# Output projection of row blocks 0 to 3 placed among the last attention head's blocks 4 to 7

## The chip, the cores and the metric

The kernel runs on one core of one Trainium2 chip. Its time is the time of one execution in microseconds (us) on the device. Unchanged, it took 1444.61 us in the median of 3 runs, which lay between 1444.29 and 1447.48 us. One further execution was taken by the hardware profiler; all durations below are of that one.

## The reference, cut to what matters

The reference is one inference step of one hybrid decoder layer, in float32. A prompt of 1024 rows with 16 meta tokens in front goes through a norm and one input projection. Its columns feed two groups: differential attention (4 heads, each with two softmax maps whose difference weights V) and a gated causal convolution with a layer norm. Both are joined again by the output projection:

```
attn_out = diff_head_out(attn_o, lw, li)
conv_out = silu(layer_norm(conv_y, cln_w, cln_b))
mix = concatenate([attn_out, conv_out], -1) @ w_out
x = x_res + rms_norm(mix, ln_mix_post)
h = rms_norm(x, ln_ffn_pre)
f = (silu(h @ w_gate) * (h @ w_up)) @ w_down
return x + rms_norm(f, ln_ffn_post)
```

Beside it eight sample sequences take one decode step each over 4096 past positions, whose keys and values lie in 256 pages of 128 rows. The keys, values and the last convolution inputs are outputs too.

## The kernel before, in words

The prompt is worked in row blocks of 128 (eight of them). Every large matmul is computed from two halves of each operand, a rounded one (H) and the rest (L), by three matmuls of 512 columns (`mm3`, lines 148 to 151): H·H, H·L, L·H. So each weight must first be loaded (SyncE, the SP queue), cast to H on ScalarE (ACT) and have its L subtracted, for the output projection on GpSimd (POOL; lines 132, 138 and 140, tiles `wo0r`, `wo0H`, `wo0L` to `wo7`), for the FFN on VectorE (DVE; lines 947, 955, 957, tiles `wr`, `wH`, `wL`).

The stages follow each other on TensorE (PE): input projection with the convolution beside it; attention of 4 heads by 8 row blocks (`attn`); output projection of 8 row blocks (`c_block`); FFN over 22 slices of the hidden width, each with three weights (gate, up, down). The decode step's work is spread over all of this in small portions: page loads on SP (line 665), products with the keys on POOL (line 679), sums on DVE (line 689), matmuls with the values on PE (`pv`, line 731).

One attention block is this chain: scores `S` on PE (lines 507, 508), taken out of PSUM on DVE with the position bias and a running minimum (line 509), `exp` on ACT (line 515), the difference of the two maps on DVE (line 526), transposes `AT` on PE (line 534), copies `ats` on ACT (line 538), products with V into `o` on PE (line 548). After blocks 3 and 7 of a head, its four blocks are normed: ACT copies `oh` and sums squares (lines 557 to 562), POOL raises to the power -1/2 (`or`, line 564), ACT scales (line 566), and `head_out` transposes on PE (`oT`, line 571), scales on ACT (line 573) and, for heads 0 to 2, stores to `mixT`. Number `od` says at which block of the next four `head_out` of the last four is issued.

`c_block(b)` reads the mix of block b (`mx`, loaded from `mixT`; for the last head straight from the tile of line 573), casts and splits it (`mH` on ACT, `mL` on DVE, lines 899 and 900), does 48 matmuls `mo` in two halves of 24, and then a chain of small norm steps on DVE, ACT and POOL (lines 909 to 918).

In the program text a loop over n = 8·head + block issues `attn`, from n = `wo0` on two loads and splits of the output projection's weights per step, and from n = 24 + `c0` on one `c_block` per step; the remaining blocks follow behind the loop. A scheduler then orders each engine's queue by its own estimate of when things can run. `slabs` is the number of 128 x 1056 float32 buffers that weights, activations and most large tiles take turns in.

Of the kernel before, what the change touches and what calls it, by code (L numbers as in the profile page):

```python
# [46 lines left out]
def tile_layer(ctx: ExitStack, tc: tile.TileContext, I, O, cfg):  # L47
# [4 lines left out]
    cst = ctx.enter_context(tc.tile_pool(name="cst", bufs=1))  # L52
    dec = ctx.enter_context(tc.tile_pool(name="dec", bufs=2))
    sm = ctx.enter_context(tc.tile_pool(name="sm", bufs=4))
    at = ctx.enter_context(tc.tile_pool(name="at", bufs=cfg["at"]))
# [379 lines left out]
    def conv_norm(b):  # L435
        pt = pdec(f"yT{b}")
        for ct in range(4):
            T.transpose(out=pt[:, ct * P : (ct + 1) * P], in_=u[ct][:, 30 + b * P : 30 + (b + 1) * P], identity=ident)
        r, nb = ln_stats(pt[:, :], P, f"ln{b}")
        for ct in range(4):  # L440
            S.activation(
                u[ct][:, 30 + b * P : 30 + (b + 1) * P], pt[:, ct * P : (ct + 1) * P], AF.Identity, scale=r, bias=nb
            )

    def conv_act(ct, half):
        pt = pdec(f"zT{ct}{half}")
        a = 30 + 512 * half
        for b in range(4):
            T.transpose(out=pt[:, b * P : (b + 1) * P], in_=u[ct][:, a + b * P : a + (b + 1) * P], identity=ident)
        S.activation(u[ct][:, a : a + 512], pt, AF.Silu, scale=clnw[:, ct : ct + 1], bias=clnb[:, ct : ct + 1])  # L450
        if half == 1:
            S.dma_start(mixT[4 + ct], u[ct][:, 30 : 30 + SEQ])
# [335 lines left out]
    def dec_step(rate):  # L788
        owed[0] += rate
        n = int(owed[0])  # L790
        owed[0] -= n
        for _ in range(n):
            if dst["done"]:
                return
            with tc.high_priority(offset=-cfg["behind"]):
                try:
                    if next(dgen) == "wait":
                        return
                except StopIteration:
                    dst["done"] = True  # L800
# [41 lines left out]
    def w_out_load(k):  # L842
        wo.append(load_split(I["w_out"][0, k * P : (k + 1) * P, :], f"wo{k}", G, n3=False))
# [3 lines left out]
    def c_start():  # L847
        C["wpost"] = slab("wpost")
        bcast_row(C["wpost"][:, :DM], I["ln_mix_post"][0])
        C["wffn"] = slab("wffn")  # L850
        bcast_row(C["wffn"][:, :DM], I["ln_ffn_pre"][0])
        C["hT"] = {}
        C["h"] = {}
        C["in"] = {}
# [24 lines left out]
    def c_load(b):  # L879
        rs = slice(b * P, (b + 1) * P)  # L880
        mx = [att(f"mx{b}{i}") for i in range(2)]
        for i in range(2):
            n = 3 + i
            D.dma_start(kn(mx[i], n), mixT[4 * i : 4 * i + n, :, rs].rearrange("c p t -> p c t"))
        xr = slab(f"xr{b}")
        D.dma_start(xr[:, :DM], I["x_prompt"][0, rs, :])
        C["in"][b] = mx, xr
# [412 lines left out]
    def chunk_to(n):  # L1300
        while emitted[0] < min(n, total):
            next(fl)
            emitted[0] += 1
            if emitted[0] == total:
                for _ in fl:
                    pass
                v_out()
                sample_v()
                sample_k()

    def c_one(b):
        if b + 1 < NB:
            c_load(b + 1)
        c_block(b)
        if b == cfg["hb"]:
            hT_chunk(0)
            for x in range(min(b, 4)):
                h_transpose(x)
        elif cfg["hb"] < b < 5:
            h_transpose(b - 1)  # L1320
        if b == cfg["w0"]:
            w_raw(0)
            w_split(0)
        if b == cfg["w1"]:
            w_raw(1)
        dec_step(cfg["rate_c"])

    nwo, ncb = 0, 0
    for n in range(NH * NB):
        h, i = n // NB, n % NB  # L1330
        chunk_to(max(9 * h + (1 if i < 2 else 2 if i < 5 else 3), 1 + int(29 * n / cfg["fend"])))
        attn(h, i)
        if cfg["cn"] <= n < cfg["cn"] + NB:
            conv_norm(n - cfg["cn"])
        if n == cfg["cn"] + NB:
            for ct in range(4):
                for half in range(2):
                    conv_act(ct, half)
        if n == cfg["scn"]:
            sample_conv()  # L1340
        if n >= cfg["wo0"]:
            for _ in range(cfg["wor"]):
                if nwo < 8:
                    w_out_load(nwo)
                    nwo += 1
                    if nwo == 8:
                        c_start()
                        c_load(0)
        if n >= 24 + cfg["c0"] and ncb < 3:
            c_one(ncb)  # L1350
            ncb += 1
        if n >= cfg["db"]:
            dec_step(cfg["rate_b"][h])
# [28 lines left out]
CFG = dict(  # L1382
    nb=3, no=1, ns=6, nd=1, nc=2,
    sqv=1, ksp=0, asp=1, sps=1,
    od=1, kt=0, ho=0,
    wd='d',
    lag=7, rlag=1, elag=2,
    xn_g=(), wi_first=1, wi_e=(13, 17), sq=0,
    behind=-400, w0=7, w1=7, wi_n=1, anchor=1, wi_v=(8, 9, 10, 11, 12), taps=11, conv=400, r2_g=1, hb=5,
    vgrp=2, fing=5, ml_g=0, fend=22, cst=0, db=3, cn=6, scn=12, wo0=27, wor=2, c0=7,  # L1390
    at=8, slabs=35, kv=4, p=6, dve_mul=0, rate_b=(1, 1.25, 1, 0.75), rate_c=1, rate_d=2.45, rate_s=2.2,
    ffn_l=lambda nc: nc.vector,
)
_INS = [
# [16 lines left out]
def build_program(inputs):  # L1411
    import numpy as np
    import concourse.bacc as bacc

    nc = bacc.Bacc("TRN2", target_bir_lowering=False, num_devices=1, dynamic_dma_scratch_size=1024)
    arrays, I, O = {}, {}, {}
    for name in _INS:
        a = np.ascontiguousarray(inputs[name])
        arrays["in_" + name] = a
        I[name] = nc.dram_tensor("in_" + name, a.shape, mybir.dt.from_np(a.dtype), kind="ExternalInput").ap()  # L1420
    for name, shape in _OUTS:
        O[name] = nc.dram_tensor("out_" + name, shape, F32, kind="ExternalOutput").ap()
    with tile.TileContext(nc, schedule_with_timeline_sim=True, auto_bufs=True) as tc:
        tile_layer(tc, I, O, CFG)
    return nc, arrays
# [8 lines left out]
```

## Time and profile before

| | |
|---|---|
| median of 3 runs | 1444.61 us |
| profiled execution | 1442.33 us |
| its span, first to last instruction | 1440.6 us |
| mean granted TensorE clock (1 is full) | 0.976 |
| PE busy | 1353.5 us (94%), 6960 matmuls |
| DVE, ACT, POOL busy | 876.8, 552.2, 560.5 us |
| the chain that ended last: PE's share | 61% |

The profiled execution is 1.7 us longer than its span, and 2.28 us shorter than the median of the runs. The first output projection matmul starts at 451.51 us of the span, the FFN's first at 548.91 us. A matmul's row shows when it started and how long it ran; consecutive ones overlap, so that a stretch is read by starts.

### The profile page before, as it was taken

Reading aid. Unit: us, or ns where it says so; the run is one execution under the profiler, and the core shown is the slowest. Engines: PE = TensorE matmul, PEld = TensorE weight load, DVE = VectorE, ACT = ScalarE, POOL = GpSimd, SP = SyncE. Lnnn points to the kernel's source line nnn. Section 1 sums busy time; section 2 is a strip of 40 time slices with the busy share of each in tenths; the row PEclk is TensorE's granted clock in tenths of the full one; section 3 lists DMA queues with packets and bytes.
Section 4 is the critical chain, followed back from the end, with each engine's and each line's share of the span. In section 5 each row is a group of like instructions: output and inputs, shape, how many; then the busy total and the mean of one; then the engine's idle time right before and its main releaser. Section 6 shows DMA issues by size and latency. Waiting matters only on the chain.

```text
span 1440.6 us, 21580 instructions
## 1 busy us (share of the span) xinstructions
PE 1353.5 (94%) x6960; PEld 1054.5 (73%) x6960; DVE 876.8 (61%) x1403; ACT 552.2 (38%) x1112; POOL 560.5 (39%) x351
## 2 busy tenths in 40 slices
PE   5999899979858999999999989999999999999997
PEld 5999799978746787777777667677676765666666
DVE  5689996945765467465748366565754265462158
ACT  7566978697855345212222121222122112211122
POOL 4598866444444123545445455454530000000023
PEclk9999999999979999999999999999999999999999
DMA  8221024226515538678777868687687656664454
GB/s 253 78 59 39 28 64 145 81 88 199 160 61 183 176 125 283 221 241 278 260 244 235 260 202 262 229 273 248 206 267 231 224 159 217 220 202 125 146 190 176
DMA packets 199678, 264.35 MB, mean 183 GB/s; under 512 B 16423, under 2 KB 99816, under 8 KB 199557
## 3 DMA queue, kind: packets, MB, share of 16 engines
q1 hardware_dynamic: 188912, 254.40, 54.1%
q10 hardware_dynamic: 10653, 8.57, 1.9%
q8 instruction: 55, 0.90, 0.3%
q14 instruction: 58, 0.48, 0.1%
HBM read 245.92 MB, written 17.48 MB: 183 GB/s over the span
## 4 chain that ended last, share of the span: by engine, by line
PE 61%; DMA 2%; issue 2%; DVE 2%; SPq 2%; POOL 1%; ACT 0%; POOLq 0%; DVEq 0%; ACTq 0%
PE pg L149 5%; PE pu L149 5%; PE pg L150 5%; PE pu L150 5%; PE pu L151 5%; PE pg L151 5%; PE dn L149 5%; PE dn L150 5%; PE dn L151 5%; PE pv L731 4%; PE mo L151 2%; PE mo L149 2%; PE mo L150 2%; DMA k<-in_cache_k 1%; POOL k L679 1%
## 5 line engine op out<-in xcount | busy, mean ns | idle before, releaser
L679 POOL TENSOR_TENSOR k<-k,qB 128x1024 f32<-128x1024 f32 x128 | 317.8, 2499 | 257.1 <-DMA k<-in_cache_k 212.0
L689 DVE TENSOR_REDUCE s<-k 128x16 f32<-128x1024 f32 x128 | 155.0, 1213 | 106.9 <-POOL k L679 106.8
L955 ACT CAST wH<-wr 128x1024 fp32r<-128x1024 f32 x66 | 69.1, 1049 | 249.1 <-DVE wL L957 142.6
L149 PE MATMUL dn<-wH,aH 128*128 128x512 f32 x352 | 141.2, 405 | 4.4 <-DVE y L998 2.7
L150 PE MATMUL dn<-wL,aH 128*128 128x512 f32 x352 | 140.9, 400 | 0.0
L149 PE MATMUL pu<-hH,wH 128*128 128x512 f32 x352 | 140.3, 399 | 0.5 <-DVE y L998 0.5
L151 PE MATMUL dn<-wH,aL 128*128 128x512 f32 x352 | 140.7, 400 | 0.0
L149 PE MATMUL pg<-hH,wH 128*128 128x512 f32 x352 | 140.4, 399 | 0.0
L151 PE MATMUL pu<-hH,wL 128*128 128x512 f32 x352 | 138.6, 395 | 1.5 <-DVE sm2n_t L123 1.5
L150 PE MATMUL pu<-hL,wH 128*128 128x512 f32 x352 | 139.5, 397 | 0.0
L150 PE MATMUL pg<-hL,wH 128*128 128x512 f32 x352 | 139.3, 396 | 0.0
L151 PE MATMUL pg<-hH,wL 128*128 128x512 f32 x352 | 139.2, 395 | 0.0
L957 DVE TENSOR_TENSOR wL<-wr,wH 128x1024 fp32r<-128x1024 f32 x66 | 97.1, 1471 | 38.0 <-ACT wH L955 21.6
L998 DVE TENSOR_TENSOR y<-dn,y 128x512 f32<-128x512 f32 x144 | 95.0, 684 | 35.4 <-PE dn L151 34.9
L414 POOL TENSOR_TENSOR cb<-cb 128x512 f32<-128x512 f32 x80 | 102.9, 1318 | 17.7 <-ACT cb L413 9.9
L423 DVE SCALAR_TENSOR_TENSOR acc<-u,cw,acc 128x512 f32<-128x512 f32 x144 | 98.8, 749 | 0.2
L1070 POOL TENSOR_TENSOR y<-y,wfpost 128x512 f32<-128x512 f32 x10 | 17.4, 1754 | 205.2 <-ACT ft L1068 205.1
L149 PEld LDWEIGHTS dn<-wH,aH 128*128 128x128 f32 x352 | 67.3, 192 | 31.2 <-DVE y L998 6.2
L981 ACT CAST aH<-sg 128x512 fp32r<-128x512 f32 x44 | 27.3, 621 | 163.2 <-DVE sg L974 163.1
L149 PEld LDWEIGHTS pu<-hH,wH 128*128 128x128 f32 x352 | 66.1, 188 | 27.8 <-issue 12.0
L149 PEld LDWEIGHTS pg<-hH,wH 128*128 128x128 f32 x352 | 66.1, 188 | 27.4 <-issue 11.6
L150 PEld LDWEIGHTS dn<-wL,aH 128*128 128x128 f32 x352 | 66.9, 190 | 25.1 <-issue 10.3
(581 smaller groups left out, 2947.3 us busy)
## 6 DMA issues: line engine op xcount, KB each, us to landing
k<-in_cache_k SPq DMA_DIRECT2D x256, 256.0 KB
v<-in_cache_v SPq DMA_DIRECT2D x256, 256.0 KB
wr<-in_w_gate SPq DMA_DIRECT2D x22, 512.0 KB
wr<-in_w_up SPq DMA_DIRECT2D x22, 512.0 KB
wr<-in_w_down SPq DMA_DIRECT2D x22, 512.0 KB
sd<-in_w_down SPq DMA_DIRECT2D x22, 512.0 KB
sw_gate<-in_w_gate SPq DMA_DIRECT2D x20, 512.0 KB
sw_up<-in_w_up SPq DMA_DIRECT2D x20, 512.0 KB
```

Of the source, the lines that this page charges most:

```text
L149: T.matmul(out, lhsT=wH, rhs=xH, start=first, stop=False)
L150: T.matmul(out, lhsT=wH, rhs=xL, start=False, stop=False)
L151: mark(T.matmul(out, lhsT=wL, rhs=xH, start=False, stop=last))
L414: G.tensor_tensor(accp, accp, t, op=ALU.add)
L423: V.scalar_tensor_tensor(dst, src, cw[:, ct, k : k + 1], acc, op0=ALU.mult, op1=ALU.add)
L679: x = G.tensor_tensor(kt, kt, qB.unsqueeze(1).to_broadcast([P, 2, 512]), op=ALU.mult)
L689: x = V.tensor_reduce(s.rearrange("p a c -> p (a c)"), kt.rearrange("p a (c d) -> p (a c) d", d=HD), axis=AX.X, op=ALU.add)
L731: x = T.matmul(pv[32 * g : 32 * g + 8, :], lhsT=a[:, q + i, :], rhs=vt[:, i, :], start=q + i < 4, stop=q + i >= NPG - 4, tile_position=(0, ...
L955: S.copy(H[:, :1024], raw[:, :1024])
L957: V.tensor_tensor(L[:, :1024], raw[:, :1024], H[:, :1024].bitcast(F32), op=ALU.subtract)
L981: S.copy(aH, sg)
L998: V.tensor_tensor(y[b][:, ws], o, y[b][:, ws], op=ALU.add)
```

## The change

Four settings and one bound in the loop are different. `c_block` is issued in the attention loop from n = 28 instead of 31 and for four row blocks (0 to 3) instead of one (the old bound of three was never reached); the weights of the output projection are issued from n = 22 (third head, block 6) instead of 27; `od` is 0, so that `head_out` of the last four blocks comes in the next block instead of the one behind it; and there are 33 slabs instead of 35.

```diff
@@ -1346,7 +1346,7 @@
                     if nwo == 8:
                         c_start()
                         c_load(0)
-        if n >= 24 + cfg["c0"] and ncb < 3:
+        if n >= 24 + cfg["c0"] and ncb < 4:
             c_one(ncb)
             ncb += 1
         if n >= cfg["db"]:
@@ -1382,13 +1382,13 @@
-    od=1, kt=0, ho=0,
+    od=0, kt=0, ho=0,
...
-    vgrp=2, fing=5, ml_g=0, fend=22, cst=0, db=3, cn=6, scn=12, wo0=27, wor=2, c0=7,
-    at=8, slabs=35, kv=4, p=6, dve_mul=0, rate_b=(1, 1.25, 1, 0.75), rate_c=1, rate_d=2.45, rate_s=2.2,
+    vgrp=2, fing=5, ml_g=0, fend=22, cst=0, db=3, cn=6, scn=12, wo0=22, wor=2, c0=4,
+    at=8, slabs=33, kv=4, p=6, dve_mul=0, rate_b=(1, 1.25, 1, 0.75), rate_c=1, rate_d=2.45, rate_s=2.2,
```

On PE, around the first output projection matmul, the queue of the kernel before reads as follows (`oT_5192` is `head_out` of the last head's blocks 0 to 3; `AT`, `o` and `ats` belong to its blocks 6 and 7; `mo` is block 0 of the output projection):

```order
L571 MATMUL oT_5192<-ident,oh_5042 128x128 x3
L548 MATMUL o_5132<-vm,metaT_115 128x128
L534 MATMUL AT_5373<-ident,p_5339 128x128 x4
L548 MATMUL o_5132<-V_4108,ats_5275 128x128 x3
L534 MATMUL AT_5381<-ident,p_5339 128x128 x4
L548 MATMUL o_5132<-V_4108,ats_5283 128x128 x4
L534 MATMUL AT_5388<-ident,p_5339 128x128
L548 MATMUL o_5132<-vm,metaT_116 128x128
L548 MATMUL o_5132<-V_4108,ats_5378 128x128 x3
L149 MATMUL mo_5430<-wo4H,mH_5420 128x512
L150 MATMUL mo_5430<-wo4L,mH_5420 128x512
L149 MATMUL mo_5457<-wo4H,mH_5420 128x512
```

The same place with the change (`oT_5178` is the same `head_out`, `pv` belongs to the decode step, `S_0_5303` is the first score tile of the last head's block 5):

```order
L731 MATMUL pv_4975<-v_0_4976,s_2014 8x512 x2
L731 MATMUL pv_4975<-v_2_5029,s_2014 8x512 x2
L571 MATMUL oT_5178<-ident,oh_5100 128x128 x4
L149 MATMUL mo_5208<-wo4H,mH_5198 128x512
L150 MATMUL mo_5208<-wo4L,mH_5198 128x512
L149 MATMUL mo_5235<-wo4H,mH_5198 128x512
L150 MATMUL mo_5235<-wo4L,mH_5198 128x512
L507 MATMUL S_0_5303<-R_30_4438,L_30_4187 128x392
L508 MATMUL S_0_5303<-R_30_4440,L_30_4187 128x392
L507 MATMUL S_392_5307<-R_30_4438,L_30_4187 128x392
L508 MATMUL S_392_5307<-R_30_4440,L_30_4187 128x392
L507 MATMUL S_0_5312<-R_31_4439,L_31_4188 128x392
```

Before, all scores, all transposes and nearly all `o` of the last head stand ahead of the first `mo`. Now all 28 score matmuls, 24 transposes and 24 `o` of its blocks 5 to 7 stand behind it, spread between the `mo` of row blocks 0 to 3.

On POOL, from the decode step's all-reduce (`dg`) to the splits of the output projection's weights, the kernel before (`k` are the products of the decode step, `or_4819` is the norm of the third head's second four blocks):

```order
L706 ISA dg_4747<-dm_4745 128x8
L140 ISA
L140 TENSOR_TENSOR wo2L<-wo2r,wo2H 128x1024
L679 TENSOR_TENSOR k_10_4718<-k_10_4718,qB_4054 128x1024
L679 TENSOR_TENSOR k_12_4825<-k_12_4825,qB_4054 128x1024
L140 TENSOR_TENSOR wo3L<-wo3r,wo3H 128x1024
L140 TENSOR_TENSOR wo4L<-wo4r,wo4H 128x1024
L564 TENSOR_TENSOR or_4819<-ssq_3939,mhalf 128x4
L140 TENSOR_TENSOR wo5L<-wo5r,wo5H 128x1024
L140 TENSOR_TENSOR wo6L<-wo6r,wo6H 128x1024
L679 TENSOR_TENSOR k_14_5067<-k_14_5067,qB_4054 128x1024
L140 TENSOR_TENSOR wo7L<-wo7r,wo7H 128x1024
```

With the change (`or_4831` is that same norm, `or_5107` that of the last head's blocks 0 to 3):

```order
L679 TENSOR_TENSOR k_10_4730<-k_10_4730,qB_4054 128x1024
L706 ISA
L706 ISA dg_4759<-dm_4757 128x8
L140 ISA
L140 TENSOR_TENSOR wo2L<-wo2r,wo2H 128x1024
L679 TENSOR_TENSOR k_12_4849<-k_12_4849,qB_4054 128x1024
L140 TENSOR_TENSOR wo3L<-wo3r,wo3H 128x1024
L564 TENSOR_TENSOR or_4831<-ssq_3939,mhalf 128x4
L140 TENSOR_TENSOR wo4L<-wo4r,wo4H 128x1024
L140 TENSOR_TENSOR wo5L<-wo5r,wo5H 128x1024
L140 TENSOR_TENSOR wo6L<-wo6r,wo6H 128x1024
L564 TENSOR_TENSOR or_5107<-ssq_4875,mhalf 128x4
```

One product moves ahead of the all-reduce, `wo4L` behind the norm, `or_5107` (before, behind `wo7L`) ahead of `wo7L` and of the product `k_14`. Three things do not show in these rows: on ACT the kernel has four more loads of an activation table (two for line 450, two for line 515), since the last SiLUs of the convolution stand among the second head's exponentials; on SP the first `mx` loads come before `wo6r`; and in the FFN, from the 13th weight on, each `wr` load stands ten page loads later in the SP queue, one weight's turn.

## Rows read from the trace of the kernel before

**Rows 1.** Windows: length; busy us (x instructions) of PE, PEld, DVE, ACT, POOL; PEclk, DMA, GB/s.

```profile
288.00:324.00 36.00, 27.44 (x173) 25.41 (x173) 15.36 (x48) 35.25 (x68) 15.66 (x11) 0.95 0.27 88
324.00:360.00 36.00, 32.89 (x233) 31.82 (x232) 19.42 (x43) 26.56 (x67) 15.10 (x7) 0.95 0.62 199
...
396.00:451.50 55.50, 33.33 (x201) 28.90 (x200) 34.71 (x77) 31.69 (x87) 26.67 (x13) 0.78 0.33 110
...
451.50:549.00 97.50, 97.50 (x462) 78.25 (x461) 52.91 (x93) 36.07 (x96) 18.23 (x19) 1.00 0.51 164
549.00:1440.00 891.00, 869.45 (x4026) 607.93 (x4024) 495.53 (x612) 188.21 (x281) 277.99 (x130) 0.99 0.68 224
```

**Rows 2.** PE's waits in 396 to 451.5: total us, times, longest.

```profile
PE S L507 <- DVE nm L509: 10.8, 3, 5.2
PE oT L571 <- ACT oh L566: 7.8, 2, 5.5
PE o L548 <- ACT ats L538: 3.5, 2, 3.2
```

**Rows 3.** Timeline of PE in 396 to 455: start, us, instruction, [idle before, releaser].

```profile
407.11 0.34 PE L507 MATMUL S<-R,L 128*128 128x392 f32 x1
407.29 0.34 PE L508 MATMUL S<-R,L 128*128 128x392 f32 x1
...
444.52 0.47 PE L571 MATMUL oT<-ident,oh 128*128 128x128 f32 x1 [5.46 <-ACT oh L566]
444.78 1.92 PE L534 MATMUL AT<-ident,p 128*128 128x128 f32 x8
...
449.69 1.06 PE L548 MATMUL o<-V,ats 128*128 128x128 f32 x8
450.59 0.27 PE L534 MATMUL AT<-ident,p 128*128 128x128 f32 x1
...
451.51 0.48 PE L149 MATMUL mo<-wo4H,mH 128*128 128x512 f32 x1
```

**Rows 4.** Timeline of POOL in 388 to 446.

```profile
400.22 0.40 POOL L706 PARTITION_ALL_REDUCE dg<-dm  x1 [7.34 <-issue]
408.57 2.37 POOL L140 TENSOR_TENSOR wo2L<-wo2r,wo2H 128x1024 fp32r<-128x1024 f32 x1 [7.95 <-ACT oh L560]
410.91 4.64 POOL L679 TENSOR_TENSOR k<-k,qB 128x1024 f32<-128x1024 f32 x2
...
420.53 1.11 POOL L564 TENSOR_TENSOR or<-ssq,mhalf 128x4 f32<-128x4 f32 x1
426.99 2.36 POOL L140 TENSOR_TENSOR wo5L<-wo5r,wo5H 128x1024 fp32r<-128x1024 f32 x1 [5.35 <-ACT wo5H L138]
```

**Rows 5.** Timeline of ACT in 408 to 452.

```profile
425.88 1.03 ACT L138 CAST wo5H<-wo5r 128x1024 fp32r<-128x1024 f32 x1
426.82 1.28 ACT L566 ACTIVATE oh<-oh,or 128x128 f32<-128x128 f32 x4
...
447.38 0.69 ACT L573 ACTIVATE mo<-oT,sublnT 128x512 f32<-128x512 f32 x1 [1.24 <-PE oT L571]
```

**Rows 6.** Timeline of DVE in 396 to 456.

```profile
415.94 4.78 DVE L526 SCALAR_TENSOR_TENSOR p<-p,cc,p 128x400 f32<-128x400 f32 x2
...
422.13 1.03 DVE L526 SCALAR_TENSOR_TENSOR p<-p,cc,p 128x400 f32<-128x400 f32 x2
...
437.73 5.43 DVE L526 SCALAR_TENSOR_TENSOR p<-p,cc,p 128x400 f32<-128x400 f32 x2
```

**Rows 7.** Groups of instructions on ACT, whole span: busy us, mean ns.

```profile
L450 ACT ACT_TABLE_LOAD x4 | 5.1, 1283 | 0.5 <-issue 0.4
```

**Rows 8.** PE's waits in 549 to 1440, and one FFN weight's load and use.

```profile
PE pv L731 <- DMA v<-in_cache_v: 5.8, 3, 4.7
...
891.04 0.39 SPq L947 DMA_DIRECT2D wr<-in_w_up  x1
...
949.04 0.39 PE L149 MATMUL pu<-hH,wH 128*128 128x512 f32 x1
```

## The prediction

> **What bounds the kernel now.** I read the windows by stage first, then PE's waits in the stage of the change, then the timelines of the engines that these waits name. In the windows [rows 1] the reader is to see three kinds of stretch. The output projection from 451.5 to 549 has PE busy for 97.50 of 97.50 us at the full granted clock, 1.00: nothing placed beside it can shorten it except by taking matmuls out of it. The FFN behind it has 869.45 of 891 us. The stretch in front, 396 to 451.5, has PE busy for only 33.33 of 55.5 us at a mean clock of 0.78, and there no engine is full: DVE 34.71, ACT 31.69, POOL 26.67. So it is bound by latency: the last head's blocks pass from engine to engine, and little other matmul work stands ready. The 22.2 us of idle PE have three sources [rows 2]: scores wait for VectorE to empty the score tiles (10.8), `head_out` waits for ACT's scaling (7.8), and products with V wait for ACT's copies (3.5).
>
> What the change can give is dense matmuls of the output projection for these holes. What it can't do is start them before their operands exist: `mo` needs `head_out` of the last head's blocks 0 to 3 and the weights' splits.
>
> **When the first `mo` comes.** Before, at 451.51 [rows 3], behind nearly the whole last head. After, the queue has it behind `oT` of blocks 0 to 3, and the longest way to that runs over POOL. There `k_10` now stands ahead of the all-reduce, which moves `dg` from 400.22 to 402.5 (one product is 4.64/2 = 2.32), and `wo2L`, which came 8.35 us behind the start of `dg` [rows 4], to 410.9. From there, with 2.36 us for a split, 2.32 for a product, 1.11 for a norm [rows 4]: `wo2L` to 413.3, `k_12` 415.6, `wo3L` 418.0, `or_4831` 419.1, `wo4L` 421.4. `wo5L` needs its cast, and on ACT that stands behind the scaling of the third head's blocks, 1.28 + 1.03 [rows 5] from about 419.2 with some copies between, so 422.5 and the split to 424.9. `wo6H` follows to about 426.2, `wo6L` to 428.6, `or_5107` to 430.2 (1.11, and half a microsecond for the handing over). Then ACT scales (1.28 [rows 5]) to 431.5, PE transposes to 432, ACT scales again (0.69) to 432.7, casts the last quarter of `mH` behind `wo7H` (1.03) to about 434.3. First `mo` 434.5: 17.0 us earlier. `wo7L` is over by 436 and the matmuls that need it come some 10 matmuls and a block of scores later, so it isn't late.
>
> **What then stands between the first `mo` and the FFN.** Before, 548.91 - 451.51 = 97.4 us [rows 1, 3]. Added are the matmuls that were ahead of it and now stand among it: 28 scores at 0.175 on average (0.18 from start to start for 392 columns [rows 3]; the shapes run from 336 to 456), 4.9; 24 transposes and 24 `o` at 0.113 ((450.59 - 449.69)/8 [rows 3]), 2.7 each; less 13 `o` that were behind it already, 1.4. Together 8.9. These are real work that loses its place in the idle stretch and takes a place in a full one: of 17 us gained, half goes back here.
>
> Two more costs. After a hole PE resumes slowly: 8 transposes took 1.92 us behind the wait of 5.46, against 1.06 for 8 like instructions 5 us later [rows 3], so about 3 us at half speed, and I put 1.5 us for the hole before `oT`. And the projection now runs closer behind what feeds it. The `mx` loads of block 2 wait for a buffer that block 1's square on ACT gives back, so its `mH` comes late by some 2.5 us; block 4 needs the last head's second `head_out`, which now ends about when block 3 does, 1 us. I take 3.5. The trace before shows no wait inside the projection; bounds are 0 (as there [rows 1]) and 7.8, the whole of `head_out`'s waits [rows 2].
>
> FFN start: 434.5 + 97.4 + 8.9 + 1.5 + 3.5 = 545.8, against 548.91: 3.1 us earlier.
>
> **Four table loads more on ACT.** 4 x 1283 ns = 5.1 us [rows 7]. They fall ahead of 288 to 324, where ACT is busy for 35.25 of 36 us, but the next 36 us have 9.4 us of idle ACT, and there PE is busy for 32.89 [rows 1], so ACT catches up. I take 0; bounds 0 and +5.1. The Trainium skill, "ScalarE: Activation LUTs", section "What ACT_TABLE_LOAD costs", gives 2.66 us to a switch, a drain of 1.38 us included; by it the four would be 10.6 us, an estimate by that page. The rows hold the 1283 ns of the load itself.
>
> **Two slabs fewer.** It is felt where slabs run out, by the FFN's weights. Each is loaded about one turn later; 66 weights in 891 us make a turn of 13.5 us. One in the middle was issued at 891.04 and first used at 949.04 [rows 8], 58 us; 44 are left, and load, cast and split need less than half of that. The first weights have little slack, but their slabs come free from the output projection's in the same order as before. I take 0. Waits of this family in the FFN today are 5.8 us, for value pages [rows 8]; as the page loads now stand ahead of the weights, they can go or double: -5.8 to +5.8.
>
> **Sum.** 1442.33 - 3.1 + 0 + 0 = 1439.2 for the profiled execution. The runs' median is 2.28 above it, so the forecast is 1441.5 us. A measurement of this kernel can tell about 0.2%, 2.9 us, from no change: the forecast lies at that edge.
>
> **Rival 1, slower: VectorE is held up by POOL.** The same instruction pair at line 526 takes 1.03 us at 422.13, between two splits, and 4.78 at 415.94 and 5.43 at 437.73 while POOL runs splits and products back to back [rows 4, 6]. Before, POOL pauses for 5.35 us ahead of `wo5L` [rows 4], in which DVE catches up. After, splits 2 to 6, a product and two norms run nearly without a pause from 411 to 430, and then `k_14`, `wo7L` and `k_16`, while DVE must work for the block that `head_out` waits for. Two more such waits in that chain cost (4.78 - 1.03) + (5.43 - 1.03) = 8.2, and as each comes with a score tile that isn't emptied, about 1 us of slow clock each: +10.2. Then the time is 1441.5 + 10.2 = 1451.7. It decides from 3.1 us on; for it speaks that the blocked rows are exactly beside the splits, against it that fewer blocks' scores are asked for in that time. The Trainium skill, "SBUF — State Buffer", section "SBUF: two separate sides", has a rule that fits: VectorE instructions with both inputs in SBUF and GpSimd share a port pair, held for a whole instruction, the other fully blocked. The rows agree in direction, with 4.78 against 1.03 us.
>
> **Rival 2, a larger gain.** The holes ahead of the first `mo` shrink too, because the scores of blocks 5 to 7 no longer hold DVE and ACT there: with `or_5107` some 7 us sooner, half of the 22.2 us [rows 2] less what I count already, another 8 us off. 1441.5 - 8 = 1433.5. For it: the 28 score matmuls of blocks 5 to 7, and with them DVE's emptying of their tiles, no longer stand ahead of `oT`. Against: my chain runs over POOL, whose 7.95 us in front of `wo2L` [rows 4] and casts don't change.
>
> **Rival 3, the wait moves.** PE now stands still in front of `oT` with nothing queued beside it, where before scores, transposes and products of blocks 5 to 7 filled part of the time. If `or_5107` comes 3 us later than I think (a weight load later on SP, which waits for slabs), all is given back: 1444.6.
>
> **Rival 4, the table loads stay on the path:** +5.1, 1446.6.
>
> **How the numbers follow.** Forecast 0.42, rival 1 0.17, rival 2 0.20, rival 3 0.15, rival 4 0.06. The forecast's own spread of some 5 us (waits of 0 to 7.8, FFN) gives 0.22 faster, 0.16 same, 0.04 slower; rival 1 0.15 slower and 0.02 same; rival 2 0.20 faster; rival 3 0.02, 0.10, 0.03; rival 4 0.04 same, 0.02 slower. Faster 0.44, same 0.32, slower 0.24. For the range I take rival 2's 1433.5 less 1.5 as the low end, 1432, since the FFN's waits can also go, and rival 1's place as the high end, 1451.
>
> **What would show it.** Right: first `mo` between 431 and 438; between it and the FFN's first matmul 109 to 114 us; FFN stretch of 891 us within 3; line 526 no longer than 5.4 us in all rows from 411 to 440. Rival 1: several rows of line 526 over 4 us, `oT` waiting past 435. Rival 2: first `mo` before 429. Rival 3: a PE hole of over 10 us in front of `oT`. Rival 4: PE waits for `exp` or `ats` between 288 and 360 grown by 5. I am wrong in kind if the FFN's length changes by more than 6 us, as I count it at nothing.

## The result: slower by 2.9%, and the profile after

The changed kernel took 1487.24 us in the median of 4 runs (1485.37 to 1490.64), the kernel before in the same comparison 1445.11 us: a ratio of 1.029, with a 95% interval of 1.027 to 1.031. I had forecast 1441.5 us with a range of 1432 to 1451. The profiled execution took 1490.64 us, with a span of 1488.9 us, 48.3 longer than before.

To see where 48.3 us went, the span is cut at four places: near the 29th and the 85th of the 112 score tiles (one and three heads' worth; 227.8 and 381.7 before, 235.5 and 414.1 after), at the first projection matmul and at the first FFN matmul. Cuts at score tiles, here and in the table of the experiments, lie up to 0.8 us from the start of the tile's first matmul (the 85th starts at 381.5 before and 414.8 after), so differences between them are good to about 1 us. The windows of the kernel after, with the same columns as [rows 1]:

```profile
0.00:235.50 235.50, 207.30 (x1276) 199.95 (x1277) 188.50 (x352) 153.97 (x296) 157.09 (x135) 0.95 0.28 85
235.50:414.10 178.60, 151.95 (x955) 143.59 (x954) 101.61 (x234) 136.18 (x333) 75.53 (x51) 0.91 0.33 106
414.10:466.00 51.90, 26.10 (x162) 22.01 (x159) 28.20 (x70) 32.28 (x88) 27.38 (x15) 0.80 0.46 151
466.00:587.70 121.70, 115.63 (x557) 93.14 (x557) 72.17 (x137) 47.12 (x122) 22.71 (x21) 0.96 0.45 151
587.70:1488.90 901.20, 869.57 (x4020) 608.91 (x4016) 497.27 (x612) 188.28 (x281) 273.01 (x130) 0.99 0.67 221
```

and the same cut of the kernel before:

```profile
0.00:227.80 227.80, 204.51 (x1282) 197.46 (x1283) 185.53 (x360) 159.19 (x306) 156.05 (x137) 0.97 0.30 90
227.80:381.70 153.90, 140.54 (x956) 134.73 (x955) 93.86 (x225) 127.29 (x319) 75.65 (x49) 0.98 0.38 119
381.70:451.50 69.80, 41.53 (x245) 36.14 (x245) 48.96 (x116) 41.49 (x111) 32.64 (x16) 0.78 0.44 146
451.50:548.90 97.40, 97.40 (x461) 78.15 (x460) 52.81 (x93) 36.07 (x96) 18.23 (x19) 1.00 0.51 164
548.90:1440.60 891.70, 869.55 (x4027) 608.03 (x4025) 495.63 (x612) 188.21 (x281) 277.99 (x130) 0.99 0.68 224
```

So 32.4 us are lost ahead of the place of the change: 7.7 up to the second head's scores, 24.7 in the second and third head (178.6 against 153.9). There nearly the same matmuls (955 and 956 rows) were busy for 11.4 us more, at a clock of 0.91 against 0.98, and PE idled 13.3 us more. From there to the first projection matmul 17.9 are gained (51.9 against 69.8), from that to the FFN 24.3 are given back (121.7 against 97.4), and the FFN is 9.5 longer. 32.4 - 17.9 + 24.3 + 9.5 = 48.3.

In the last head one wait stands out on PE, which was two of 2.34 and 5.46 us before:

```profile
450.04 0.48 PE L571 MATMUL oT<-ident,oh 128*128 128x128 f32 x1 [14.78 <-ACT oh L566]
...
466.04 0.79 PE L149 MATMUL mo<-wo4H,mH 128*128 128x512 f32 x1 [2.23 <-ACT mH L899]
```

It is `head_out` of the third head's second four blocks. Its norm (`or`) comes late on POOL:

```profile
424.97 2.92 POOL L679 TENSOR_TENSOR k<-k,qB 128x1024 f32<-128x1024 f32 x1
433.49 0.39 POOL L706 PARTITION_ALL_REDUCE dg<-dm  x1 [5.60 <-PE o L548]
441.25 2.33 POOL L140 TENSOR_TENSOR wo2L<-wo2r,wo2H 128x1024 fp32r<-128x1024 f32 x1 [7.36 <-issue]
...
448.16 1.39 POOL L564 TENSOR_TENSOR or<-ssq,mhalf 128x4 f32<-128x4 f32 x1
```

and ACT, which should have delivered the squares for it and the exponentials, stood still too:

```profile
443.61 1.04 ACT L138 CAST wo3H<-wo3r 128x1024 fp32r<-128x1024 f32 x1 [5.99 <-POOL wo2L L140]
444.56 0.31 ACT L562 ACTIVATE junk<-oh 128x129 f32<-128x129 f32 x1
444.77 0.19 ACT L562 ACTIVATION_READ_ACCUMULATOR junk<-oh 128x1 f32 x1
444.87 0.83 ACT L515 ACTIVATE p<-p,nm 128x656 f32<-128x656 f32 x1
```

The cast of `wo3` waits for POOL's split of `wo2`, and that one comes behind POOL's empty 7.36 us after the all-reduce. What stands behind it on ACT, squares of `oh` and exponentials, waits until 443.6, and DVE with it. Then the scaling waits for the norm that stands behind `wo3L`.

### The profile page after: what moved, and what is told of

The parts are those of the page before. It is cut to its first block, busy times and chain, and to the rows that moved or that the text cites. A ratio compares the mean times of both kernels' runs of the same rounds, so it can differ in the third digit from the quotient of the medians.

```text
span 1488.9 us, 21586 instructions
## 1 busy us (share of the span) xinstructions
PE 1370.6 (92%) x6960; PEld 1067.6 (72%) x6960; DVE 887.7 (60%) x1403; ACT 557.8 (37%) x1116; POOL 555.7 (37%) x351
## 3 DMA queue, kind: packets, MB, share of 16 engines
q1 hardware_dynamic: 188912, 254.40, 51.9%
## 4 chain that ended last, share of the span: by engine, by line
PE 49%; DVE 5%; SPq 5%; DMA 4%; issue 4%; POOL 2%; ACT 1%; DVEq 0%; POOLq 0%
PE pu L151 4%; PE pu L149 4%; PE pu L150 4%; PE pg L149 4%; PE pg L150 4%; PE pg L151 4%; PE dn L149 4%; PE dn L150 3%; PE dn L151 3%; PE pv L731 3%; SPq L665 2%; SPq L659 2%; PE mo L151 2%; PE mo L149 2%; DMA v<-in_cache_v 2%
## 5 line engine op out<-in xcount | busy, mean ns | idle before, releaser
L957 DVE TENSOR_TENSOR wL<-wr,wH 128x1024 fp32r<-128x1024 f32 x66 | 97.4, 1476 | 50.8 <-ACT wH L955 24.3
L151 PEld LDWEIGHTS pu<-hH,wL 128*128 128x128 f32 x352 | 66.4, 189 | 25.0 <-issue 6.9
```

The source lines that it names most:

```text
L151: mark(T.matmul(out, lhsT=wL, rhs=xH, start=False, stop=last))
L957: V.tensor_tensor(L[:, :1024], raw[:, :1024], H[:, :1024].bitcast(F32), op=ALU.subtract)
```

## The experiments

One table holds all runs: place of the 85th score tile, first projection matmul, first FFN matmul and FFN length in the profiled execution (us of the span), and the median time with its ratio to the kernel before in the same comparison.

| run | 85th score | first mo | FFN start | FFN | median | ratio, interval |
|---|---|---|---|---|---|---|
| before | 381.7 | 451.5 | 548.9 | 891.7 | 1445.11 | |
| after | 414.1 | 466.0 | 587.7 | 901.2 | 1487.24 | 1.029, 1.027 to 1.031 |
| 33 slabs | 396.6 | 461.1 | 565.6 | 901.2 | 1466.89 | 1.015, 1.010 to 1.019 |
| 33, weights early | 398.5 | 455.3 | 566.6 | 903.0 | 1468.59 | 1.015, 1.010 to 1.019 |
| all but the blocks | 411.4 | 463.2 | 583.9 | 896.4 | 1487.57 | 1.030, 1.025 to 1.034 |
| od = 0, 35 slabs | 385.6 | 451.0 | 547.6 | 897.1 | 1445.76 | 1.001, 0.998 to 1.003 |
| od = 0, 33 slabs | 407.8 | 474.4 | 578.0 | 896.2 | 1474.65 | 1.020, 1.016 to 1.023 |
| after with od = 1 | 397.6 | 449.2 | 564.8 | 897.4 | 1463.37 | 1.013, 1.011 to 1.015 |
| after at 35, p 5, at 6 | 386.3 | 439.8 | 556.5 | 944.7 | 1500.17 | 1.038, 1.034 to 1.041 |
| before with p 5, at 6 | 376.7 | 446.4 | 543.8 | 940.4 | 1485.54 | 1.029, 1.027 to 1.031 |
| 34 slabs | 388.6 | 454.0 | 555.2 | 909.4 | 1465.94 | 1.014, 1.011 to 1.018 |
| od = 1, 34 slabs | 386.9 | 442.1 | 550.2 | 904.9 | 1459.80 | 1.012, 1.008 to 1.016 |
| after, splits on DVE | 414.0 | 459.5 | 578.0 | 897.4 | 1476.27 | 1.021, 1.019 to 1.024 |
| od = 1, 34, splits on DVE | 384.2 | 429.0 | 537.5 | 902.2 | 1448.17 | 1.003, 1.001 to 1.006 |
| blocks from n = 30, 35 | 388.2 | 447.1 | 550.5 | 901.2 | 1445.14 | 0.999, 0.998 to 1.001 |
| weights early, DVE, 35 | 383.4 | 434.5 | 545.4 | 893.5 | 1440.43 | 0.997, 0.995 to 0.998 |

(The places are those of one execution each. The profiled one took 1453.39 us in the last row but one, 8 above its median, and 1441.44 with od = 1, 34 slabs and the splits on DVE, 7 below.)

**33 slabs alone**, to the kernel before:

```diff
-    at=8, slabs=35, kv=4, p=6,
+    at=8, slabs=33, kv=4, p=6,
```

> The kernel before with 33 slabs instead of 35 and nothing else. Theory S (the loss was made ahead of the change's place: with two buffers fewer the input weights and tiles of the second and third head come late): score matmuls of the third head 20 to 35 us later than before, and the FFN longer by 5 to 12 us; the time 1470 to 1490 us. Theory O (the loss comes from head_out one block earlier, and from the order that follows from it: SiLUs of the convolution among the second head's exponentials): this run within 6 us of before, 1439 to 1451 us.

20.5 us slower than the kernel before in its own comparison (1446.40), half of the loss of 42. The FFN is 9.5 us longer, as theory S had it; the 85th score tile is 14.9 us late, less than its 20 to 35, and the time 3 us below its range. Theory O had expected no loss and is out for this half.

**33 slabs and early weights** (`wo0=22`):

> The kernel before with 33 slabs and the output projection's weights issued from n = 22. Theory S: no more than 6 us from the run with 33 slabs alone, since the weights' loads wait for buffers in any case. Theory W (the early weights take 16 buffers for their halves away from the last two heads): 10 us or more slower than with 33 slabs alone, scores of the last head later by as much. Theory O: within 6 us of before.

1.7 us from the run before: theory W is out. The first projection matmul comes 5.8 us sooner, the FFN doesn't.

**All but the blocks** (the changed kernel with `c0=7`):

> The changed kernel with the projection's blocks put back to n = 31 (c0 = 7): 33 slabs, weights from n = 22, head_out one block earlier. Theory S: most of the 42 us is here already, 1470 to 1490 us, and the first projection matmul comes later than in the changed kernel by up to 17 us while the FFN starts at about the same time. Theory O: as slow as the changed kernel less what the blocks' place costs, and clearly slower than the run with 33 slabs and early weights. Theory P (the blocks among the last head are what costs): 1440 to 1455 us.

1487.57, as slow as the changed kernel. But this run doesn't undo the whole move: with early weights the scheduler puts 17 transposes and 34 rows of `o` behind the first projection matmul by itself, and with `od = 0` as well, as here, 24 and 48, as many as in the changed kernel. The 28 scores go back in front of it, and `head_out` of the last head's blocks 0 to 3 comes behind it; the sum hasn't moved. 19 us lie between this run and the one before, which differ by `od` alone.

**od = 0 alone, at 35 slabs:**

> The kernel before with head_out one block earlier (od = 0), 35 slabs, nothing else. Theory O: 15 to 35 us slower than before, with a wait of PE on ACT's scaling of over 10 us in each head. Theory S: within 8 us of before, 1437 to 1453 us.

No difference. So theory O is out as stated: an earlier `head_out` costs only together with fewer slabs.

**od = 0 and 33 slabs:**

> The kernel before with 33 slabs and head_out one block earlier; weights and blocks as before. Theory X (head_out one block earlier costs nothing with 35 slabs and some 19 us with 33, for it makes the heads denser in live buffers): 1480 to 1492 us. Theory Y (the 19 us between the second and third run need the early weights too): 1463 to 1472 us, like 33 slabs alone.

1474.65, between the two: 8 us above 33 slabs alone, not 19. Neither theory has it; the rest of the 19 us needs the early weights as well. Against `od = 0` with 35 slabs (1445.76), two slabs cost some 29 us here, and none of them in the FFN, which is 896.2 against 897.1 us long.

**The changed kernel with od = 1** (and `c0=5`, since the last head's first four blocks are finished one step later):

```diff
-    od=0, kt=0, ho=0,
+    od=1, kt=0, ho=0,
```

> The changed kernel with head_out put back (od = 1) and therefore the projection's blocks from n = 29, not 28: 33 slabs, weights from n = 22. Theory X: 1462 to 1473 us, as with 33 slabs and early weights. If the place of the blocks gains by itself (my term of 17 us less what goes back), 1455 to 1465 us. Theory P (the blocks among the last head cost): over 1475 us.

1463.37: 24 us faster than the changed kernel and 5.2 faster than 33 slabs with early weights (1468.59, in another comparison, whose before was 2 us higher). Both the range of theory X and that of a gain by the blocks hold 1463.37, and the two ratios' intervals, 1.011 to 1.015 and 1.010 to 1.019, overlap: if blocks among the last head gain a few us when `head_out` doesn't come in between, this doesn't show it clear of noise.

**The change with 35 slabs, paid for by other pools, and its control:**

```diff
-    at=8, slabs=33, kv=4, p=6,
+    at=6, slabs=35, kv=4, p=5,
```

> The changed kernel with 35 slabs, paid for by one score buffer (p = 5 instead of 6) and two smaller attention buffers (at = 6 instead of 8). Theory S: most of the loss goes away; within 10 us of the next run, which has the same buffers without the change, and 1440 to 1465 us. Theory P: still 1475 us or more, 25 us above the next run.

> Control to the run before: the kernel before with p = 5 and at = 6, 35 slabs. 1443 to 1455 us, as the heads wait seldom for score buffers; if it is over 1460 us, the smaller pools cost as much as slabs do.

My control was wrong: the smaller pools cost 41 us alone, all of it in the FFN (940.4 us), so the time against the kernel before says little. Against its control the change is 14.6 us slower (1500.17 to 1485.54), more than the 10 that theory S allowed and less than the 25 of theory P: the 85th score tile comes 9.6 us later than in the control, the first projection matmul 6.6 us sooner, the first FFN matmul 12.7 us later. So a part of the loss is there with 35 slabs too, if the smaller pools don't make it. The rest goes: the change reaches the 85th score tile at 386.3, where with 33 slabs it was 414.1.

**34 slabs alone:**

> The kernel before with 34 slabs instead of 35, nothing else. If every slab counts (each shortens the lead of the weights in the heads and in the FFN): 1452 to 1460 us, about half of the 21 us that two slabs cost. If there is a point below which it breaks: within 4 us of before, or like 33 slabs, 1463 to 1471 us.

1465.94, like 33. It isn't a price by the slab. The loss is divided otherwise: 6.9 us up to the 85th score tile, 17.7 in the FFN.

**od = 1 with 34 slabs**, and **the L splits on DVE** (to the changed kernel, and to this one):

```diff
-        wo.append(load_split(I["w_out"][0, k * P : (k + 1) * P, :], f"wo{k}", G, n3=False))
+        wo.append(load_split(I["w_out"][0, k * P : (k + 1) * P, :], f"wo{k}", V, n3=False))
```

> The changed kernel with od = 1, therefore the projection's blocks from n = 29, and 34 slabs. If the blocks' place gains the 5 us that it seemed to gain at 33 slabs (1463.4 against 1468.6 us), 3 to 7 us below the run with 34 slabs alone; if that gain was chance of the order, within 3 us of it or slower.

> The changed kernel with the eight L splits of the projection's weights on DVE instead of POOL. Theory H (in the last head, ACT's cast of wo3 waits for a slab that POOL's split of wo2 gives back behind its 7.36 us without work around the all-reduce, and with it wait the exponentials, the norm and oT): PE's wait of 14.8 us in front of oT falls below 8 us, the first projection matmul comes 5 to 12 us earlier, 1475 to 1483 us. Rival: the norm itself is bound by POOL's all-reduce, or DVE becomes the bound with 8 splits more: the wait stays over 10 us or another takes its place, 1485 to 1495 us.

> Od = 1, blocks from n = 29, 34 slabs and the L splits on DVE: all that helped so far together. If the gains add, 1440 to 1452 us, which could be below the kernel before; if DVE's splits take from the score tiles what POOL's pause cost, like the run with 34 slabs and od = 1, within 4 us.

The first gave 1459.80, 6 us below 34 slabs alone, as expected, though the intervals overlap (1.008 to 1.016 and 1.011 to 1.018) and the two differ in the early weights too. The second tests the stall in the last head, and theory H holds but for one bound: 11 us less than the changed kernel, the first projection matmul 6.5 us sooner, and the wait in front of `oT` at 8.14 instead of 14.78, where it had said below 8. In it ACT's cast of `wo3` waits 0.31 us for DVE:

```profile
431.59 1.04 ACT L138 CAST wo3H<-wo3r 128x1024 fp32r<-128x1024 f32 x1 [0.31 <-DVE wo2L L140]
```

The norm is still behind the all-reduce's pause, so 8 us stay, as the rival had said of the norm. The third, with 1448.17, is 11.6 us below the first, so the gains add; in the profiled execution its FFN starts 11.4 us before that of the kernel before, and is 10.5 us longer.

**Parts of the change with all 35 slabs.** By `od=0`, blocks from n = 30 (`c0=6`, two blocks in the loop); and by `od=0`, `wo0=22` with the splits on DVE. The full change at 35 slabs with the other pools untouched was not run.

> The kernel before with od = 0 and the projection's blocks from n = 30 (two of them in the attention loop instead of one), with all 35 slabs; weights from n = 27 as before. If only the missing slabs made the change slow: 1436 to 1446 us, with the FFN within 6 us of the 891.7 us before. If head_out one block earlier with blocks among the last head costs with all slabs too: 1450 to 1465 us, first projection matmul later than 451 us or a hole in front of oT over 10 us.

> The kernel before with od = 0, the weights from n = 22 and their L splits on DVE, with all 35 slabs; blocks as before. If only the missing slabs made the change slow: 1436 to 1448 us, heads within 8 us of before. If early weights and early head_out fill the slabs in the heads whatever their number: third head's scores 15 us or more late and 1455 to 1475 us.

Blocks earlier at 35 slabs: no difference (0.999), though its FFN is 9.5 us longer, not within 6, in the one execution profiled. Weights early: 0.997, interval 0.995 to 0.998, faster than both kernels, with `od = 0` and early weights in it, which cost some 20 us at 33 slabs. It has the splits on DVE besides, worth 11 us in the two pairs above, so the slabs' number and the splits' engine aren't told apart in it. Its windows, from the 85th score tile on, as cut above:

```profile
383.40:434.50 51.10, 33.32 (x195) 28.87 (x193) 41.82 (x120) 37.89 (x100) 10.80 (x7) 0.85 0.45 149
434.50:545.40 110.90, 107.40 (x513) 87.50 (x513) 57.32 (x99) 40.47 (x109) 21.33 (x20) 0.96 0.50 165
545.40:1438.90 893.50, 870.14 (x4027) 608.68 (x4025) 495.90 (x612) 188.40 (x281) 277.23 (x130) 0.99 0.67 223
```

POOL has 10.80 us of work in the first piece, where it had 32.64 over 69.8 us before. And the first projection matmul comes at 434.5, 17.0 us sooner than before, with the blocks not moved in the program: the scheduler has placed it ahead of 17 of the last head's transposes all the same.

## Why the prediction was wrong, point by point

**Two slabs fewer: "I take 0", bounds -5.8 to +5.8. This step failed.** Alone they cost 20.5 us (33 slabs alone), and some 29 with `od = 0`. I looked for their price only in the FFN and as a shorter lead of weights that have lead to spare. Two things were missing.

First, the FFN. The SP queue is worked in order, and page loads stand behind weight loads. A weight load that waits for a slab holds up the pages behind it, and these have little lead. The longest case in the kernel after, on SP and on PE:

```profile
721.29 0.39 SPq L947 DMA_DIRECT2D wr<-in_w_up  x1
721.93 2.03 SPq L665 DMA_DIRECT2D v<-in_cache_v  x4
...
728.60 1.89 PE L731 MATMUL pv<-v,s 128*8 128x512 f32 x8 [7.03 <-DMA v<-in_cache_v]
```

This is the FFN's 14th weight load. It waits 7.5 us for a slab that DVE's split gives back, the value pages are issued 0.6 us behind it, and PE stands still for 7.03 us until they are there. With 33 slabs alone the same load waits 7.3 us, and PE 8.20 behind it; before, this load doesn't wait. SP's waits for the FFN's weight loads, of which a slab given back by DVE's split is the largest part, in the kernel before (total us, times, longest):

```profile
SPq L947 <- DVE wL L957: 9.9, 5, 2.9
SPq L945 <- DVE wL L957: 9.6, 1, 9.6
SPq L945 <- PE dn L151: 2.9, 1, 2.9
```

and with 33 slabs alone:

```profile
SPq L947 <- DVE wL L957: 18.3, 7, 7.3
SPq L945 <- DVE wL L957: 14.8, 2, 11.4
SPq L947 <- PE dn L151: 11.6, 2, 8.5
```

Over all rows of lines 945 and 947 that is 26 us before, 52 with 33 slabs, 94 with 34 and 28 in the fastest kernel; the FFN is 891.7, 901.2, 909.4 and 893.5 us long, in the same order. The other runs don't keep this order: with `od = 1`, 34 slabs and the splits on DVE it is 95 us for an FFN of 902.2, with blocks from n = 30 and 35 slabs 28 us for 901.2, and with `od = 0` 29 us at 35 slabs and 43 at 33 for 897.1 and 896.2. So a weight load's wait counts where pages that PE needs next stand behind it, and its sum is no measure of the FFN's length; nor do fewer slabs lengthen the FFN in every pair.

PE's waits for value pages, `pv`, were 5.8 us before [rows 8]; in the kernel after:

```profile
PE pv L731 <- DMA v<-in_cache_v: 12.0, 8, 7.0
```

So my bound of +5.8, a doubling of that wait, was just passed by this row (+6.2), which is two thirds of the FFN's 9.5 us. The rest is other idle time of PE, as its busy time stayed the same (869.55 and 869.57 in the windows). My "turn later" was right in the weights and of little use: PE waits only 0.3 us in all for a weight's split there.

Second, and larger, the heads, which I did not price at all. The input projection's weights for the next heads take the same slabs. The load of one of them, the third stripe's `wi11` (first and last start of each instruction; before, then with 33 slabs):

```profile
L132 SPq DMA_DIRECT2D wi11r<-in_w_in x1: 389/389/389, 276.9 to 276.9; - x1
...
L151 PE MATMUL pv<-xH,wi11L x24: 287/337/417, 296.7 to 328.2; 128*128 128x384 f32 x16, 128*128 128x280 f32 x8
```

```profile
L132 SPq DMA_DIRECT2D wi11r<-in_w_in x1: 389/389/389, 306.9 to 306.9; - x1
...
L151 PE MATMUL pv<-xH,wi11L x24: 289/338/522, 315.3 to 341.1; 128*128 128x384 f32 x16, 128*128 128x280 f32 x8
```

It is issued 30 us later, after 26.9 us in which SP waits for a slab that the score matmuls of line 508 give back (before, this load waits for none), its lead falls from 19.8 to 8.4 us, and PE waits for its split. The direct wait is small (0.7 us). In the second and third head PE is busy for 144.79 of 162.8 us with 947 matmuls at a clock of 0.94, where it was 140.54 of 153.9 with 956 at 0.98:

```profile
233.80:396.60 162.80, 144.79 (x947) 137.96 (x947) 91.06 (x222) 132.96 (x327) 73.95 (x50) 0.94 0.37 114
```

I take it that less projection work is queued when the attention waits. That the missing weights cause all of this is argued from these rows; that slabs cause it is shown by the runs, at `od = 1` and at `od = 0`. Nor do the runs settle why 34 and 33 slabs cost the same in the sum while they divide it differently (6.9 and 14.9 us before the 85th score tile): every number of slabs also gives another order.

**The earlier `head_out`: counted inside my chain, no price of its own.** At 35 slabs that is right (1.001). With 33 slabs and early weights it costs 19 us (1468.59 to 1487.57); in the profiled executions the 85th score tile comes 12.9 us later (398.5 to 411.4) and the first FFN matmul 17.3. Together the parts lose more than apart. For the second head's part I have no row that names its cause; it is left open.

**The first `mo`, 17.0 us earlier: the distance was right, the reason only in part.** From the 85th score tile on it came 17.9 us sooner than before; by the clock it came 14.5 later, since that stretch began 32.4 late. The chain behind the all-reduce held: from the start of `dg` to the first `mo` I had 32.0 us (402.5 to 434.5), and it took 32.6 (433.49 to 466.04), with `wo2L` 7.76 us behind the start of `dg`, 8.35 before [rows 4]. But I had it that `mo` needs `head_out` of the last head's blocks 0 to 3, and the first ones don't: of the 24 in a half only the last three, those with `wo3`, read the last head. In the run with all but the blocks the first `mo` stands ahead of that `head_out` (`mo` at 463.19, `oT` at 474.80) and comes 51.8 us after the 85th score tile, as early as here. So I gave to the blocks' place what the early weights and the scheduler bring without it, and that the distance came out is luck to that extent. And I followed POOL alone. ACT's `wo3H` waits for POOL's `wo2L`, and I priced nothing behind it, though squares, exponentials and DVE's work stand behind it in order: that is the hole of 14.78 us, rival 3's place ("a PE hole of over 10 us in front of `oT`") by another wait than a late load. With that wait gone (splits on DVE) the kernel is 11 us faster.

**Between first `mo` and FFN: 111.3 us expected, 121.7 measured.** Mis-sized in three terms. The matmuls added there are 95 (the 557 of the window hold the FFN's first one, the 461 before don't), where I had counted 28 + 24 + 24 - 13 = 63: 35 `o` and 8 `pv` are added instead of 11 and none, 3.6 us at 0.113 each. The count of `o` mixed two units: the 24 are products of the program, and each of them is two rows in the trace (352 rows of line 548 for 176 transposed tiles), while the 13 are rows. PE idled 6.1 us, where I had 3.5 for waits. And at a mean clock of 0.96 some 4.9 us are lost, an estimate (0.04 of 121.7), against the 1.5 I put. The three make 9.6 of the 10.4 us. The order of the sizes was right: what dense work gains in the idle stretch is given back in the full one, -17.9 and +24.3 for my -17.0 and +13.9; but the run with all but the blocks has -18.0 and +23.3, so neither is the moved blocks' own.

**Rival 1**, VectorE held up by POOL: not the cause of that hole. From 396 to 470 one row of line 526 is over 4 us, where before two were, 4.78 and 5.43 [rows 6], and during the hole in front of `oT` DVE itself stands idle for ACT:

```profile
422.84 5.22 DVE L526 SCALAR_TENSOR_TENSOR p<-p,cc,p 128x640 f32<-128x640 f32 x2
...
445.82 0.16 DVE L521 RECIPROCAL rl<-l 128x1 f32<-128x1 f32 x1 [6.17 <-ACT p L515]
...
446.32 2.70 DVE L526 SCALAR_TENSOR_TENSOR p<-p,cc,p 128x400 f32<-128x400 f32 x2
```

The Trainium skill, "SBUF — State Buffer", section "SBUF: two separate sides", still fits what is seen: with the splits on DVE the longest pair of that line between 418 and 462 takes 1.73 us. **Rival 4**, the table loads: four more are there (14 against 10 at lines 450 and 515, 5.1 us); in the run with 33 slabs alone three more are, so their own price isn't told apart there. But with 34 slabs there are two fewer (8), and that run is as slow as the one with 33: they aren't what makes it slow.

## What to carry to other kernels

A buffer that is taken away has to be priced at every stage that draws from its pool, and also at what waits behind the waiting load in the same queue: in the FFN here, page loads of the decode step, not the load itself. When a change takes memory from another pool, run the memory's price alone before anything else; it was half of the loss here, and with all slabs parts of the same change were neutral or faster, though the whole of it was still 14.6 us slower than its control at 35 slabs. Look, too, at what the scheduler has already moved before crediting a gain to the setting that was meant to move it. And a wait found in a queue is priced by everything that stands behind it on that engine, not by its own row.

## What the runs showed of the hardware that I had not expected

The clock's part was nearly as large as that of idle time. Up to the FFN, PE's idle time grew by 21.8 us from before to after (64.9 to 86.7, the four stretches of the windows added), and the busy time of nearly the same matmuls by 17.0 us (484.0 to 501.0), with a granted clock of 0.91 instead of 0.98 in the second and third head and 0.96 instead of 1.00 in the projection. Length times (1 - clock), added over the four windows, grows from 25.3 to 43.1 us, which as an estimate covers the 17.0. With 33 slabs alone it was 3.4 us more idle time and 13.3 more busy time; there the waits cost less by themselves than the slower work did. That the waits bring the slower work is not shown apart from these sums; one case of it is the row at 728.60 above, where eight `pv` take 1.89 us behind PE's wait of 7.03, against 1.04 us for eight of them at 692.33 in the kernel before.
